# A long convolution through two half-size transforms at odd frequencies, with the last filter product stacked in fp32r

## The chip, the core and the metric

The kernel runs on one core of a Trainium2 chip. The metric is the device time of one execution in microseconds (us). It is one long program: a first transformer block, then two layers of a second block whose mixer has an attention branch and a long-convolution branch (hyena). Nearly all of its time is matrix work on TensorE (PE in the profile); the vector engine (DVE), the scalar engine (ACT) and the weight loads issued by SyncE (SP) work beside it.

## What is computed

The change touches the long convolution of the second block, which runs in layer 0 for two streams (the latent tokens and the context, 256 tokens each) and in layer 1 for one. Cut to what matters:

```python
def hyena_filter(length, fw1, fb1, fw2, fb2, fw3, fb3, fw4, freq):
    ...
    h = jnp.sin(freq[0] * (z @ fw1 + fb1))
    h = jnp.sin(freq[1] * (h @ fw2 + fb2))
    h = jnp.sin(freq[2] * (h @ fw3 + fb3))
    h = (h @ fw4).reshape(length, 2, HYENA_WIDTH)      # 64 -> 2 x 512 channels
    ...
    h = h * decay[:, None, :]
    return h[:, 0], h[:, 1]

def bidirectional_long_conv(v, h_fwd, h_bwd):
    length = v.shape[1]                                # 256
    n_fft = 2 * length
    k = jnp.concatenate([h_fwd, jnp.zeros((1, HYENA_WIDTH), h_fwd.dtype), h_bwd[:0:-1]], axis=0)
    v_f = jnp.fft.rfft(v.astype(jnp.float32), n=n_fft, axis=1)
    k_f = jnp.fft.rfft(k, n=n_fft, axis=0)
    return jnp.fft.irfft(v_f * k_f[None], n=n_fft, axis=1)[:, :length]

def hyena_mix(u, conv_w, conv_b, ..., bias):
    x0, x1, v = jnp.split(short_conv(u, conv_w, conv_b), 3, axis=-1)
    v = v * x1
    h_fwd, h_bwd = hyena_filter(length, ...)
    y = bidirectional_long_conv(v, h_fwd, h_bwd) + v.astype(jnp.float32) * bias
    return (y * x0).astype(u.dtype)
```

The filter depends on weights only, so its spectrum can be worked out long before the layer needs it.

## The kernel before

**Products.** Every large fp32 product is three fp32r matmuls: an operand is split into hi (an ACT copy that rounds to fp32r) and lo (a DVE subtract), and hi·hi, hi·lo and lo·hi are summed in PSUM. Weights come from DRAM as `raw` tiles of 512 KB (two k-tiles, issued on SP at L111); ACT copies each half to `whi` (L115), DVE makes `wlo` (L116). `gemm` (L126 to L128) and `gemm_T` (L139 to L141) use them. The pieces of the convolution go through `put`/`hilo` (L190 on ACT, L191 on DVE) and `mm3` (L215 to L217).

**The filter's spectrum.** `spectrum(layer)` is a generator. Three small fp32 matmuls `fm`, each followed by a sine (`sin`, 64 partitions x 256 points), give `sinh`. The last product with `fw4` (64 x 1024) is one fp32 matmul for each of two time halves and two directions (`hf` L763, `hb` L767); the trace shows such an fp32 matmul as two records. Then sums and differences are split into `hs` and `hd`, and `K` is their transform by the constant `F` (1024 columns: 256 cosines with the Nyquist row packed in, 256 sines): four products of six matmuls, and six more, `Kn`, for the Nyquist row. ACT or DVE evicts to `KR`, `KI`, and `KD` is `KR` with its first row exchanged. `spectrum_jobs` cuts the generator into 12 jobs; a background list releases them inside other matmul streams as these spend their columns. So spectrum 0 lies in the second feed-forward part of the first block (some 373 to 504 us), spectrum 1 in the feed-forward part of layer 0 (some 1205 to 1304 us).

**The convolution of a stream.** `hyena` makes three projections (`hy`), each followed by a three-tap convolution (`conv`: one ACT, two DVE instructions). `turn_v` transposes `vv` (`trv`, 8 transposes a stream) and splits it into `vTh`/`vTl`. `forward` transforms it: for each of two frequency halves m, real and imaginary part, 2 time halves x 3 matmuls into a `V` tile of 512 channels, 24 matmuls in all; DVE multiplies by `KR`, `KI`, `KD` and combines (L864 to L869, L854), and the four results are split into `Yh`/`Yl`. `inverse` is 48 matmuls `iy` of 256 columns with the constant `G`, and an elementwise end that gives `hyo`. Forwards run three times: twice in layer 0 (first matmuls at 615.9 and 649.8 us) and once in layer 1 (1384.6 us). Around them stand the gates' products (`ga`, `gh`) and, after the convolution, `oh` = hyo · w_o_hyena.

**What sets the order.** The kernel is written with tile pools; a scheduler fixes the order of each engine's instructions ahead of time by a model of its own. Each engine and the SP queue then run their row in that order and wait for semaphores. A tile pool bounds how far ahead a producer may run: 4 `raw` tiles, 16 `whi` and 16 `wlo`, 6 PSUM tiles for products (`mm`) and 2 for transposes and spectra (`tr`).

Of the kernel before, what the change touches and what calls it, by code (L numbers as in the profile page):

```python
# [42 lines left out]
class Net:  # L43
# [546 lines left out]
    def block1(self, nxt, before):  # L590
# [3 lines left out]
        self.fcols = self.const.tile([64, 12], F32, name="fcols")  # L594
# [128 lines left out]
    def sin(self, ps, b, fr):  # L723

        nc = self.nc
        x, n = self.k2("sarg", [64, 256]), self.k2("sn", [64, 256])
        nc.vector.tensor_scalar(out=x, in0=ps, scalar1=b, scalar2=fr, op0=ALU.add, op1=ALU.mult)
        nc.vector.tensor_scalar(out=n, in0=x, scalar1=1.0 / (2.0 * math.pi), scalar2=MAGIC, op0=ALU.mult, op1=ALU.add)
        nc.vector.tensor_scalar(out=n, in0=n, scalar1=MAGIC, scalar2=None, op0=ALU.subtract)
        for c in TWO_PI:  # L730
            nc.vector.scalar_tensor_tensor(out=x, in0=n, scalar=-c, in1=x, op0=ALU.mult, op1=ALU.add)
        nc.vector.tensor_scalar(out=x, in0=x, scalar1=PI_IN, scalar2=-PI_IN, op0=ALU.min, op1=ALU.max)
        h = self.k2("sinh", [64, 256])
# [3 lines left out]
    def spectrum(self, layer):  # L737

        nc, a = self.nc, self.a
# [9 lines left out]
        h = z  # L749
        for i in range(3):  # L750
            ps = self.tr("fm")
            nc.tensor.matmul(ps[:64, :256], w1 if i == 0 else w23[:, i - 1, :], h, start=True, stop=True)
            h = self.sin(ps[:64, :256], self.fcols[:, fc + i:fc + i + 1], self.fcols[:, fc + 3 + i:fc + 4 + i])
            yield
        dec = self.k4("dec", [P, 2, 512])
        nc.sync.dma_start(dec, a["decay"])
        F = self.const_pair("F", "dft")
        hs, hd = [self.pair(self.k4, x, [P, 2, 512]) for x in ("hs", "hd")]
        ALL = slice(None)
        for t in range(2):  # L760
            f, b = self.k2("f", [P, 512]), self.k2("b", [P, 512])
            ps = self.tr("hf")
            nc.tensor.matmul(ps, h[:, t * P:(t + 1) * P], w4[:, 0:512], start=True, stop=True)  # L763
# [3 lines left out]
            nc.tensor.matmul(ps, h[:, t * P:(t + 1) * P], w4[:, 512:1024], start=True, stop=True)  # L767
# [10 lines left out]
        KR, KI, KD = self.k4("KR", [P, 2, 512]), self.k4("KI", [P, 2, 512]), self.k2("KD", [P, 512])  # L778
        for m in range(4):
            ps = self.tr("K")  # L780
            src = hs if m < 2 else hd
            for t in range(2):
                self.mm3(ps, F, (ALL, slice(t * 512 + m * P, t * 512 + (m + 1) * P)), src, (ALL, t), t == 0, t == 1)
            if m == 2:
                nc.vector.tensor_scalar(out=KI[:, 0, :], in0=ps, scalar1=self.mask0, scalar2=None, op0=ALU.mult)
            else:
                nc.scalar.activation((KR if m < 2 else KI)[:, m % 2, :], ps, AF.Copy)
# [4 lines left out]
        nc.vector.tensor_copy(KD, KR[:, 0, :])  # L792
        nc.vector.tensor_copy(KD[:1, :], ps[:1, :])
        self.spectra[layer] = KR, KI, KD

    def spectrum_jobs(self, layer):
        g = self.spectrum(layer)
        return [(("spec", layer), lambda: next(g, None))] * 12

    def hyena(self, layer, X, between):  # L800
# [39 lines left out]
        KR, KI, KD = self.spectra[layer]  # L840
# [9 lines left out]
        def forward(vT):  # L850
# [5 lines left out]

            for m in range(2):
                V = [self.mm("V"), self.mm("V")]
                for q in range(2):
# [4 lines left out]
                nc.vector.tensor_tensor(out=t1, in0=V[0], in1=KR[:, m, :], op=ALU.mult)  # L864
                nc.vector.tensor_tensor(out=t2, in0=V[1], in1=KI[:, m, :], op=ALU.mult)
                comb(m, 0, t1, t2, ALU.subtract)
                t3, t4 = self.k2("y3", [P, 512]), self.k2("y4", [P, 512])
                nc.vector.tensor_tensor(out=t3, in0=V[0], in1=KI[:, m, :], op=ALU.mult)
                nc.vector.tensor_tensor(out=t4, in0=V[1], in1=KD if m == 0 else KR[:, 1, :], op=ALU.mult)  # L869
                comb(m, 1, t3, t4, ALU.add)  # L870
# [497 lines left out]
def dft_consts():  # L1368
    n = np.arange(256)[:, None]
    f = np.arange(256)[None]  # L1370
    th = 2 * np.pi * ((n * f) % 512) / 512
    fwd = np.concatenate([np.cos(th), -np.sin(th)], axis=1)
    fwd[:, 256] = (-1.0) ** np.arange(256)
    inv = 2 * fwd.T / 512
# [108 lines left out]
```

## Time and profile before

| | |
|---|---|
| median of 3 runs | 1786.92 us (1786.06 to 1790.84) |
| the profiled execution's own time | 1782.49 us |
| its span in the trace | 1780.7 us |
| PE busy | 1741.6 us, 98% of the span |
| DVE / ACT / PEld busy | 1238.5 / 864.3 / 1511.5 us |
| granted TensorE clock | full (0.998 in the mean) |

The profiled execution is 4.4 us faster than the median of the runs, so sums are made against 1782.49 and the difference is carried to the median. Matmul records overlap (their ends are modelled): the cost of one in a stream is the distance between starts, not the duration printed. The rows come further down, in groups.

### The profile page before, as it was taken

The numbers are of one execution on the slowest core, as the hardware profiler recorded it, in microseconds if no ns is written. First come the engines' busy times: TensorE is split into PE (matmuls) and PEld (weight loads), VectorE is DVE, ScalarE is ACT, GpSimd is POOL, SyncE is SP. The second block draws the span as 40 slices with busy tenths as digits, with TensorE's granted clock in tenths as the row PEclk, the third lists the DMA queues.
The fourth block names the chain that finished last, engine by engine and source line by source line (L and its number), as shares of the span: only waits on it lengthen the run. The fifth ranks groups of instructions, "written<-read, shape, count | busy, mean of one in ns | idle before, by whom it ended". The sixth has DMA issues, their size and how long they took to land.

```text
span 1780.7 us, 26970 instructions
## 1 busy us (share of the span) xinstructions
PE 1741.6 (98%) x9982; PEld 1511.5 (85%) x9982; DVE 1238.5 (70%) x2447; ACT 864.3 (49%) x1807; POOL 49.0 (3%) x77
## 2 busy tenths in 40 slices
PE   7999999999999999999999999999999999999998
PEld 5998887889888888888888888888789998989997
DVE  5855778886568887687667886456548857775554
ACT  6544557654467442356525433332336446565443
POOL 0000000000001000010000000000000001000000
PEclk9999999999999999999999999999999999999999
DMA  7757544675454428432545566454234554465553
GB/s 263 276 188 250 173 145 143 227 244 169 152 189 167 156 92 291 135 107 77 183 160 184 194 220 247 159 218 163 85 129 154 175 174 129 160 214 192 190 201 114
DMA packets 96244, 315.65 MB, mean 177 GB/s; under 512 B 10942, under 2 KB 18544, under 8 KB 96112
## 3 DMA queue, kind: packets, MB, share of 16 engines
q1 hardware_dynamic: 94176, 309.70, 51.1%
q10 hardware_dynamic: 1936, 4.23, 0.7%
q8 instruction: 78, 1.28, 0.3%
q14 instruction: 54, 0.44, 0.1%
HBM read 301.25 MB, written 12.63 MB: 176 GB/s over the span
## 4 chain that ended last, share of the span: by engine, by line
PE 83%; DMA 6%; DVE 6%; ACT 2%; issue 1%; POOL 1%; SPq 0%; POOLq 0%; ACTq 0%; DVEq 0%
PE f2u L139 3%; PE f2dn L126 3%; PE f2u L140 3%; PE f2u L141 3%; PE f2g L139 3%; PE f2g L140 3%; PE f2g L141 3%; PE f2dn L128 3%; PE f2dn L127 3%; DVE wlo L116 2%; PE O L1102 2%; PE trP L185 1%; PE oa L141 1%; PE oa L140 1%; PE oa L139 1%
## 5 line engine op out<-in xcount | busy, mean ns | idle before, releaser
L116 DVE TENSOR_TENSOR wlo<-raw,whi 128x512 fp32r<-128x512 f32 x844 | 546.4, 682 | 163.0 <-ACT whi L115 130.3
L115 ACT ACTIVATE whi<-raw 128x512 fp32r<-128x512 f32 x844 | 494.4, 624 | 164.6 <-PE f2dn L128 41.1
L648 DVE SCALAR_TENSOR_TENSOR wmod<-wmod,crow 128x1024 f32<-128x1024 f32 x96 | 116.0, 1218 | 1.0 <-DMA wmod<-in_w_modT_dram 0.6
L126 PE MATMUL f2dn<-whi,f2ah 128*128 128x512 f32 x264 | 103.7, 393 | 0.0
L139 PE MATMUL f2u<-fxh,whi 128*128 128x512 f32 (+1 forms) x304 | 103.2, 340 | 0.0
L139 PE MATMUL f2g<-fxh,whi 128*128 128x512 f32 (+1 forms) x304 | 103.2, 340 | 0.0
L141 PE MATMUL f2u<-fxh,wlo 128*128 128x512 f32 (+1 forms) x304 | 103.0, 339 | 0.0
L141 PE MATMUL f2g<-fxh,wlo 128*128 128x512 f32 (+1 forms) x304 | 103.0, 339 | 0.0
L140 PE MATMUL f2g<-fxl,whi 128*128 128x512 f32 (+1 forms) x304 | 103.0, 339 | 0.0
L140 PE MATMUL f2u<-fxl,whi 128*128 128x512 f32 (+1 forms) x304 | 103.0, 339 | 0.0
L128 PE MATMUL f2dn<-whi,f2al 128*128 128x512 f32 x264 | 102.8, 390 | 0.0
L127 PE MATMUL f2dn<-wlo,f2ah 128*128 128x512 f32 x264 | 102.8, 389 | 0.0
L648 DVE SCALAR_TENSOR_TENSOR mjunk<-wmod,crow 128x1024 bf16<-128x1024 f32 x64 | 77.5, 1218 | 22.0 <-DMA wmod<-in_w_modT_dram 18.3
L141 PE MATMUL hy<-lxh,wlo 128*128 128x256 f32 (+1 forms) x224 | 69.6, 315 | 0.1
L140 PE MATMUL hy<-lxl,whi 128*128 128x256 f32 (+1 forms) x224 | 69.7, 315 | 0.0
L139 PE MATMUL hy<-lxh,whi 128*128 128x256 f32 (+1 forms) x224 | 69.1, 315 | 0.0
L280 ACT ACTIVATE f2s<-f2g 128x512 f32<-128x512 f32 (+1 forms) x38 | 18.9, 496 | 99.5 <-PE f2g L141 99.5
L190 ACT ACTIVATE f2ah<-f2s 128x512 fp32r<-128x512 f32 (+1 forms) x40 | 21.3, 532 | 92.9 <-DVE f2s L283 92.9
L283 DVE TENSOR_TENSOR f2s<-f2u,f2s 128x512 f32<-128x512 f32 (+1 forms) x38 | 21.3, 562 | 63.4 <-PE f2u L141 63.4
L139 PEld LDWEIGHTS f2u<-fxh,whi 128*128 128x128 f32 x304 | 57.6, 190 | 7.6 <-issue 1.5
L139 PEld LDWEIGHTS f2g<-fxh,whi 128*128 128x128 f32 x304 | 57.7, 190 | 7.2 <-issue 0.9
L141 PEld LDWEIGHTS f2u<-fxh,wlo 128*128 128x128 f32 x304 | 57.7, 190 | 6.3
(520 smaller groups left out, 4809.1 us busy)
## 6 DMA issues: line engine op xcount, KB each, us to landing
wmod<-in_w_modT_dram SPq DMA_DIRECT2D x96, 512.0 KB, 5.9
raw<-in_ffn_w_gu_dram SPq DMA_DIRECT2D x88, 512.0 KB, 5.2
raw<-in_w_gate_up_dram SPq DMA_DIRECT2D x88, 512.0 KB, 5.7
raw<-in_w_in_dram SPq DMA_DIRECT2D x80, 512.0 KB, 4.4
raw<-in_ffn_w_down_dram SPq DMA_DIRECT2D x44, 512.0 KB, 5.1
raw<-in_w_down_dram SPq DMA_DIRECT2D x44, 512.0 KB, 4.0
raw<-in_w_out_dram SPq DMA_DIRECT2D x24, 512.0 KB, 4.7
raw<-in_w_in_q_dram SPq DMA_DIRECT2D x16, 512.0 KB, 3.8
```

The lines of the kernel that those rows point to most:

```text
L115: nc.scalar.activation(hi, raw[:, j], AF.Copy)
L116: nc.vector.tensor_tensor(out=lo, in0=raw[:, j], in1=hi.bitcast(F32), op=ALU.subtract)
L126: nc.tensor.matmul(ps[:, :n], xh, hi, start=first and k == 0, stop=False)
L127: nc.tensor.matmul(ps[:, :n], xh, lo, start=False, stop=False)
L128: nc.tensor.matmul(ps[:, :n], xl, hi, start=False, stop=last and k == z)
L139: nc.tensor.matmul(ps[:, m], hi[:, c], xh, start=first and k == 0, stop=False)
L140: nc.tensor.matmul(ps[:, m], hi[:, c], xl, start=False, stop=False)
L141: nc.tensor.matmul(ps[:, m], lo[:, c], xh, start=False, stop=last and k == z)
L190: nc.scalar.activation(hi, ps, AF.Copy)
L283: nc.vector.tensor_tensor(out=s, in0=pu[:, :W], in1=s, op=ALU.mult)
L648: nc.vector.scalar_tensor_tensor(out=junk, in0=w, scalar=1.0, in1=self.crows[s], op0=ALU.mult, op1=ALU.mult, accum_out=self.modc[layer][s] ...
L1102: nc.tensor.matmul(po[:, :256], V[:, kt, g * P:(g + 1) * P], pT[:, k, :], start=k == 0, stop=k == nt - 1)
```

## The change

The transform is taken at the odd frequencies, (k + 1/2) of 512, of which a real sequence of 256 has 256 and none is special: no Nyquist row, no mask, no `KD`. Even and odd samples are transformed separately at 128 frequencies, with 128 samples each; the value at frequency k and the one at its mirror image are the sum and the difference of the two halves. So a forward transform is 2 (real, imaginary) x 2 (even, odd) x 3 matmuls, and the same for each of `hs` and `hd`. `halves` joins the two: ACT copies the odd part out of PSUM (`odd`), DVE adds and subtracts. Transposes read `vv` with a stride of two samples; the constant `F` is 512 columns wide, its hi and lo in one tile.

The last filter product becomes fp32r: sine layer 3 runs on 128 partitions (its weights stand twice side by side), so that `h` stands twice; `hh` keeps hi in partitions 0 to 63 and lo in 64 to 127, and `w4`, loaded twice, one copy under the other, is split into hi and lo. Two matmuls, `hh` by w4 hi and by w4 lo, give (hi + lo) · (hi + lo). The spectrum becomes 11 jobs.

```diff
@@ const_pair
-        p = self.pair(self.k4, name, [P, D])
-        f = self.k4(name + "f", [P, D])
+        n = int(np.prod(self.a[src].shape[1:])) // 512
+        if n == 1:
+            both = self.k4(name, [P, 2, 512], F32R)
+            p = both[:, 0, :], both[:, 1, :]
+        else:
+            p = self.pair(self.k4, name, [P, n * 512])
+        f = self.k4(name + "f", [P, n * 512])
...
@@ spectrum
+        ws = [w1, w23[:, 0, :], w23[:, 1:3, :]]
         for i in range(3):
+            n = P if i == 2 else 64
             ps = self.tr("fm")
-            nc.tensor.matmul(ps[:64, :256], w1 if i == 0 else w23[:, i - 1, :], h, start=True, stop=True)
+            nc.tensor.matmul(ps[:n, :256], ws[i], h, start=True, stop=True)
...
+        hh = self.k2("hh", [P, 256], F32R)
+        nc.scalar.activation(hh, h, AF.Copy)
+        nc.vector.tensor_tensor(out=hh[64:], in0=h[64:], in1=hh[64:].bitcast(F32), op=ALU.subtract)
+        wp = self.pair(self.k4, "fw", [P, D])
...
+        for q in range(2):
+            c = slice(512 * q, 512 * q + 512)
+            self.put(wp, (slice(None), c), w4[:, c])
...
+        def filt(ps, t, q):
+            for i in range(2):
+                nc.tensor.matmul(ps, hh[:, t * P:(t + 1) * P], wp[i][:, q * 512:(q + 1) * 512], start=i == 0, stop=i == 1)
...
-            nc.tensor.matmul(ps, h[:, t * P:(t + 1) * P], w4[:, 0:512], start=True, stop=True)
+            filt(ps, t, 0)
...
-        KR, KI, KD = self.k4("KR", [P, 2, 512]), self.k4("KI", [P, 2, 512]), self.k2("KD", [P, 512])
-        for m in range(4):
-            ps = self.tr("K")
-            src = hs if m < 2 else hd
+        KR, KI = self.k4("KR", [P, 2, 512]), self.k4("KI", [P, 2, 512])
+        for q, (src, K) in enumerate(((hs, KR), (hd, KI))):
+            ps = [self.tr("K") for _ in range(2)]
             for t in range(2):
-                self.mm3(ps, F, (ALL, slice(t * 512 + m * P, t * 512 + (m + 1) * P)), src, (ALL, t), t == 0, t == 1)
...
+                self.mm3(ps[t], F, (ALL, slice(t * 256 + q * P, t * 256 + (q + 1) * P)), src, (ALL, t), True, True)
+            self.halves(K[:, 0, :], K[:, 1, :], ps[0], ps[1], q)
             yield
-        ps = self.tr("Kn")
-        for t in range(2):
-            self.mm3(ps[:1, :], F, (ALL, slice(t * 512 + 256, t * 512 + 257)), hs, (ALL, t), t == 0, t == 1)
...
+    def halves(self, a, b, even, odd, imag):
+        o = self.k2("odd", [P, 512])
+        nc.scalar.activation(o, odd, AF.Copy)
+        nc.vector.tensor_tensor(out=a, in0=even, in1=o, op=ALU.add)
+        if imag:
+            nc.vector.tensor_tensor(out=b, in0=o, in1=even, op=ALU.subtract)
+        else:
+            nc.vector.tensor_tensor(out=b, in0=even, in1=o, op=ALU.subtract)
@@ hyena, turn_v
-                    self.transpose(ps[:, ct * P:(ct + 1) * P], vv[ct][:, s * 256 + t * P:s * 256 + (t + 1) * P])
+                    self.transpose(ps[:, ct * P:(ct + 1) * P], vv[ct][:, s * 256:(s + 1) * 256].rearrange("p (l e) -> p e l", e=2)[:, t, :])
@@ hyena, forward
+            V = [[self.mm("V") for _ in range(2)] for _ in range(2)]
+            A = []
+            for q in range(2):
+                for t in range(2):
+                    o = t * 256 + q * P
+                    self.mm3(V[q][t], F, (ALL, slice(o, o + P)), vT, (ALL, t), True, True)
+            for q in range(2):
+                A.append([self.k2("y1", [P, 512]), self.k2("y2", [P, 512])])
+                self.halves(*A[q], *V[q], q)
             for m in range(2):
-                V = [self.mm("V"), self.mm("V")]
-                for q in range(2):
-                    for t in range(2):
-                        o = q * 256 + m * P
-                        self.mm3(V[q], F, (ALL, slice(t * 512 + o, t * 512 + o + P)), vT, (ALL, t), t == 0, t == 1)
-                t1, t2 = self.k2("y1", [P, 512]), self.k2("y2", [P, 512])
...
+                re, im = A[0][m], A[1][m]
                 t3, t4 = self.k2("y3", [P, 512]), self.k2("y4", [P, 512])
...
+                nc.vector.tensor_tensor(out=t3, in0=re, in1=KI[:, m, :], op=ALU.mult)
+                nc.vector.tensor_tensor(out=re, in0=re, in1=KR[:, m, :], op=ALU.mult)
+                nc.vector.tensor_tensor(out=t4, in0=im, in1=KI[:, m, :], op=ALU.mult)
+                comb(m, 0, re, t4, ALU.subtract)
+                nc.vector.tensor_tensor(out=im, in0=im, in1=KR[:, m, :], op=ALU.mult)
+                comb(m, 1, t3, im, ALU.add)
```

The order changes near these pieces only. On ACT around the forward transform of layer 1, before (from the split of the transposed `vv` to the last `Yh`; `x_...` is the three-tap convolution of the third projection):

```order
L190 ACTIVATE vTh<-trv 128x512 x2
L813 ACTIVATE x_14020<-hy,cols 128x256
L115 ACTIVATE whi<-raw 128x512 x4
L190 ACTIVATE Yh<-y_14181 128x512
L813 ACTIVATE x_14020<-hy,cols 128x256
L190 ACTIVATE Yh<-y_14188 128x512
L190 ACTIVATE Yh<-y_14209 128x512
L190 ACTIVATE Yh<-y_14216 128x512
```

and after:

```order
L190 ACTIVATE vTh<-trv 128x512 x2
L839 ACTIVATE x_13990<-hy,cols 128x256
L115 ACTIVATE whi<-raw 128x512 x3
L815 ACTIVATE odd<-V 128x512
L115 ACTIVATE whi<-raw 128x512
L815 ACTIVATE odd<-V 128x512
L839 ACTIVATE x_13990<-hy,cols 128x256
L115 ACTIVATE whi<-raw 128x512 x2
L190 ACTIVATE Yh<-y_14153 128x512
L190 ACTIVATE Yh<-y_14165 128x512
L190 ACTIVATE Yh<-y_14154 128x512
L190 ACTIVATE Yh<-y_14177 128x512
```

Two `odd` copies are new, the first of them behind three `whi` copies; all four `Yh` now stand behind six `whi` copies where the first stood behind four.

On DVE at the same place, before (from the first product with the spectrum):

```order
L864 TENSOR_TENSOR y_14181<-V,KR 128x512
L865 TENSOR_TENSOR y_14182<-V,KI 128x512
L868 TENSOR_TENSOR y_14188<-V,KI 128x512
L854 TENSOR_TENSOR y_14181<-y_14181,y_14182 128x512
L869 TENSOR_TENSOR y_14189<-V,KD 128x512
L864 TENSOR_TENSOR y_14209<-V,KR 128x512
L191 TENSOR_TENSOR Yl<-y_14181,Yh 128x512
```

and after:

```order
L816 TENSOR_TENSOR y_14153<-V,odd 128x512
L820 TENSOR_TENSOR y_14154<-V,odd 128x512
L816 TENSOR_TENSOR y_14159<-V,odd 128x512
L818 TENSOR_TENSOR y_14160<-odd,V 128x512
L895 TENSOR_TENSOR y_14165<-y_14153,KI 128x512
L897 TENSOR_TENSOR y_14166<-y_14159,KI 128x512
L896 TENSOR_TENSOR y_14153<-y_14153,KR 128x512
L899 TENSOR_TENSOR y_14159<-y_14159,KR 128x512
L880 TENSOR_TENSOR y_14153<-y_14153,y_14166 128x512
L880 TENSOR_TENSOR y_14165<-y_14165,y_14159 128x512
```

Four additions and subtractions stand ahead of the first product, and the first combination (L880, L854 before) is the ninth instruction instead of the fourth.

On SP somewhat later in layer 1 (`spill` stores a gate's tile to DRAM; the numbers tell tiles apart), before:

```order
L1205 DMA spill_14318<-Ta_14316 128x256
L1205 DMA spill_14347<-Ta_14345 128x256
L1205 DMA spill_14376<-Ta_14374 128x256
L111 DMA raw_14519<-in_w_o_hyena_dram 128x1024
L1205 DMA spill_14405<-Ta_14403 128x256
L111 DMA raw_14529<-in_w_o_hyena_dram 128x1024
```

and after:

```order
L1235 DMA spill_14284<-Ta_14282 128x256
L1235 DMA spill_14313<-Ta_14311 128x256
L1235 DMA spill_14342<-Ta_14340 128x256
L1235 DMA spill_14371<-Ta_14369 128x256
L111 DMA raw_14485<-in_w_o_hyena_dram 128x1024
L111 DMA raw_14495<-in_w_o_hyena_dram 128x1024
```

The first load of w_o_hyena stands behind the fourth spill instead of the third.

## Rows read from the trace of the kernel before

**Rows 1.** The page's parts 1 and 4: busy time; the chain that ended last.

```profile
PE 1741.6 (98%) x9982; PEld 1511.5 (85%) x9982; DVE 1238.5 (70%) x2447; ACT 864.3 (49%) x1807; POOL 49.0 (3%) x77
...
PE 83%; DMA 6%; DVE 6%; ACT 2%; issue 1%; POOL 1%; SPq 0%; POOLq 0%; ACTq 0%; DVEq 0%
```

**Rows 2.** Waits of PE: waiter, releaser: us in total, times, longest.

```profile
PE trm L185 <- DVE ffn1n L697: 10.2, 2, 9.8
```

**Rows 3.** Windows: us, busy (count) of PE, PEld, DVE, ACT, POOL, clock, DMA, GB/s.

```profile
400.00:440.00 40.00, 40.00 (x306) 36.81 (x305) 26.32 (x52) 19.27 (x41) 0.00 (x0) 1.00 0.48 160
600.00:640.00 40.00, 38.38 (x200) 32.74 (x199) 33.55 (x58) 14.86 (x26) 0.00 (x0) 1.00 0.36 117
1260.00:1310.00 50.00, 50.00 (x215) 39.00 (x214) 20.07 (x32) 15.22 (x26) 0.00 (x0) 1.00 0.27 89
1370.00:1420.00 50.00, 48.61 (x375) 46.63 (x375) 45.68 (x89) 27.37 (x55) 0.00 (x0) 1.00 0.46 150
```

**Rows 4.** PE's timeline in spectrum 0, one product K: start, duration, instruction.

```profile
458.06 0.39 PE L215 MATMUL K<-hsh,Fh 128*128 128x512 f32 x1
...
459.42 0.39 PE L126 MATMUL ffn2dn<-whi,ffn2ah 128*128 128x512 f32 x1
```

**Rows 5.** Instructions of single tiles: count, duration ns min/median/max, first and last start.

```profile
L215 PE MATMUL K<-hsh,Fh x8: 389/389/389, 458.1 to 1284.1; 128*128 128x512 f32 x8
...
L215 PE MATMUL V<-vTh,Fh x24: 389/389/497, 615.9 to 1390.2; 128*128 128x512 f32 x24
...
L763 PE MATMUL hf<-fw,sinh x8: 589/641/693, 415.0 to 1265.8; 64*128 64x512 f32 x8
...
L185 PEld LDWEIGHTS trv<-ident,vv x24: 138/140/144, 607.5 to 1381.6; 128*128 128x128 f32 x24
```

**Rows 6.** PE's timeline around one product hf of spectrum 0 and of spectrum 1.

```profile
414.71 0.28 PE L140 MATMUL ffn2u<-ffn2l,whi 128*128 128x256 f32 x1
414.83 0.28 PE L141 MATMUL ffn2u<-ffn2h,wlo 128*128 128x256 f32 x1
415.04 1.12 PE L763 MATMUL hf<-fw,sinh 64*128 64x512 f32 x2
...
416.31 0.28 PE L140 MATMUL ffn2u<-ffn2l,whi 128*128 128x256 f32 x1
...
1252.14 0.39 PE L128 MATMUL f2dn<-whi,f2al 128*128 128x512 f32 x1
...
1253.85 0.39 PE L127 MATMUL f2dn<-wlo,f2ah 128*128 128x512 f32 x1
```

**Rows 7.** PE's timeline, the Nyquist product Kn of spectrum 0.

```profile
500.81 0.40 PE L215 MATMUL Kn<-hsh,Fh 128*1 128x512 f32 x1
...
502.20 0.28 PE L139 MATMUL ffn2u<-ffn2h,whi 128*128 128x256 f32 x1
```

**Rows 8.** Groups by line and shape, DVE, 600 to 660 us: busy, mean ns, idle before.

```profile
L854 DVE TENSOR_TENSOR y<-y,y 128x512 f32<-128x512 f32 x7 | 4.8, 682 | 0.0
```

**Rows 9.** Timelines of DVE and of PE, layer 0: last Yl, first iy.

```profile
629.52 0.69 DVE L191 TENSOR_TENSOR Yl<-y,Yh 128x512 fp32r<-128x512 f32 x1
...
633.12 0.28 PE L215 MATMUL iy<-Gh,Yh 128*128 128x256 f32 x1
```

**Rows 10.** ACT's timeline in layer 1; in brackets idle before and its releaser.

```profile
1388.40 1.15 ACT L115 ACTIVATE whi<-raw 128x512 fp32r<-128x512 f32 x2 [1.06 <-DMA raw<-in_w_in_dram]
...
1397.85 0.63 ACT L190 ACTIVATE Yh<-y 128x512 fp32r<-128x512 f32 x1 [1.56 <-DVE y L854]
```

**Rows 11.** PE's timeline in layer 1: end of V, first iy, start and end of gh's part.

```profile
1390.63 0.39 PE L217 MATMUL V<-vTh,Fl 128*128 128x512 f32 x1
1390.86 0.28 PE L139 MATMUL hy<-lxh,whi 128*128 128x256 f32 x1
...
1398.29 0.28 PE L215 MATMUL iy<-Gh,Yh 128*128 128x256 f32 x1
...
1410.29 0.28 PE L139 MATMUL gh<-lxh,whi 128*128 128x256 f32 x1
...
1419.54 0.28 PE L139 MATMUL oh<-hyoh,whi 128*128 128x256 f32 x1
```

**Rows 12.** SP's timeline in layer 1: the fourth spill, the last load of w_o_hyena.

```profile
1407.89 0.32 SPq L1205 DMA_DIRECT2D spill<-Ta  x1
1408.31 0.38 SPq L111 DMA_DIRECT2D raw<-in_w_o_hyena_dram  x1
```

More of the change, by code (lines that the diff above doesn't have):

```diff
@@ L199, in const_pair @@
     def const_pair(self, name, src):
-        p = self.pair(self.k4, name, [P, D])
-        f = self.k4(name + "f", [P, D])
+        n = int(np.prod(self.a[src].shape[1:])) // 512
[5 more added lines that the diff above has]
+        f = self.k4(name + "f", [P, n * 512])
         self.nc.sync.dma_start(f, self.a[src].rearrange("p a b -> p (a b)"))
-        for q in range(2):
+        for q in range(n):
             c = slice(512 * q, 512 * q + 512)
@@ L593, in block1 @@
         hs = {}
-        self.fcols = self.const.tile([64, 12], F32, name="fcols")
+        self.fcols = self.const.tile([P, 12], F32, name="fcols")
         for t in range(2):
@@ L742, in spectrum @@
         nc.sync.dma_start(w1, a["filt_w1"][layer])
-        w23 = self.k2("fw23", [64, 2, 64])
+        w23 = self.k2("fw23", [64, 3, 64])
         nc.sync.dma_start(w23, a["filt_w23"][layer])
-        w4 = self.k4("fw4", [P, D])[:64, :]
+        w4 = self.k4("fw4", [P, D])
         nc.sync.dma_start(w4, a["filt_w4"][layer])
@@ L766, in spectrum @@
             ps = self.tr("hb")
-            nc.tensor.matmul(ps, h[:, t * P:(t + 1) * P], w4[:, 512:1024], start=True, stop=True)
+            filt(ps, t, 1)
             if t == 0:
@@ L777, in spectrum @@
             yield
[L778 to L781 removed]
+        KR, KI = self.k4("KR", [P, 2, 512]), self.k4("KI", [P, 2, 512])
+        for q, (src, K) in enumerate(((hs, KR), (hd, KI))):
+            ps = [self.tr("K") for _ in range(2)]
             for t in range(2):
[L783 to L794 removed]
+                self.mm3(ps[t], F, (ALL, slice(t * 256 + q * P, t * 256 + (q + 1) * P)), src, (ALL, t), True, True)
+            self.halves(K[:, 0, :], K[:, 1, :], ps[0], ps[1], q)
+            yield
+        self.spectra[layer] = KR, KI
+    def halves(self, a, b, even, odd, imag):
+        nc = self.nc
+        o = self.k2("odd", [P, 512])
[5 more added lines that the diff above has]
+            nc.vector.tensor_tensor(out=b, in0=even, in1=o, op=ALU.subtract)
     def spectrum_jobs(self, layer):
         g = self.spectrum(layer)
[L798 removed]
+        return [(("spec", layer), lambda: next(g, None))] * 11
     def hyena(self, layer, X, between):
@@ L839, in hyena @@
         self.need(("spec", layer))
-        KR, KI, KD = self.spectra[layer]
+        KR, KI = self.spectra[layer]
         def turn_v(s):
@@ L1368, in dft_consts @@
 def dft_consts():
[L1369 to L1374, printed above, removed]
-    inv[0] /= 2
-    inv[256] /= 2
-    part = lambda x: np.ascontiguousarray(x.reshape(-1, P, x.shape[1]).transpose(1, 0, 2).astype(np.float32))
-    return part(fwd), part(inv)
+    th = 2 * np.pi * (np.arange(P) + 0.5) / 512
+    n = np.arange(256).reshape(P, 2).T
+    fwd = np.stack([np.concatenate([np.cos(n[p][:, None] * th), -np.sin(n[p][:, None] * th)], axis=1) for p in range(2)], axis=1)
+    t = np.arange(256)[None]
+    thm = [th[:, None], np.pi - th[:, None]]
+    inv = np.stack([f(m * t) / 256 for f in (np.cos, lambda x: -np.sin(x)) for m in thm], axis=1)
+    return np.ascontiguousarray(fwd.astype(np.float32)), np.ascontiguousarray(inv.astype(np.float32))
 def hyena_consts():
```

31 lines of the change are left out of this document (14 added, 17 removed).

## The prediction, written before the run

> **What bounds the kernel now.** The page first: PE is busy for 98% of the span, and the chain that ended last runs 83% through PE, 6% through DVE and 6% through transfers [rows 1]. The list of PE's waits next: the largest is 10.2 us in two places where a feed-forward part begins, far from this change, and no wait of the spectra stands in the list [rows 2]. Then the stretches that the change touches, as windows: around spectrum 0 and spectrum 1 PE is busy for all of 40.00 and 50.00 us while DVE is busy for 26.32 and 20.07; around the first forwards of layer 0 PE has 38.38 of 40, DVE 33.55; around the forward of layer 1 PE has 48.61 of 50 and DVE 45.68 [rows 3]. The granted clock is 1.00 in all four. So in the spectra a matmul taken away is worth its distance to the next start, nearly certainly. In layer 0 DVE has some slack, in layer 1 hardly any: there the saving may be taken back by DVE, ACT or a transfer.
>
> **The price of a matmul.** The six matmuls of a K product start at 458.06 and the next matmul after them at 459.42: 1.36 / 6 = 0.2267 us each [rows 4]. The printed 389 ns overlap.
>
> **What goes, term by term.** (1) K: before, 48 matmuls in two layers (8 in each of the six groups of which one is shown [rows 5]); the change makes 2 x 2 x 3 a layer, 24 in all. 24 x 0.2267 = 5.44 us. (2) V: 72 matmuls (three groups of 24 [rows 5]) become 36: 36 x 0.2267 = 8.16. (3) The Nyquist product goes: 500.81 to 502.20 is 1.39 [rows 7], twice: 2.78. (4) The last filter product: from 414.83 to 416.31 stand hf and two matmuls of 256 columns at the 0.12 of 414.71 to 414.83, so 1.48 - 0.24 = 1.24; from 1252.14 to 1253.85 stand hf and two of 512 columns, 1.71 - 0.45 = 1.26 [rows 6]. Eight such products at 1.25; the new one is two fp32r matmuls of 512 columns, which I price like K's, 0.453: 8 x 0.797 = 6.37. They are new in one respect, operands whose partitions 64 to 127 hold another part of the same number; TensorE reads 128 rows there as in K. Sum: 22.75 us.
>
> **What comes in.** DVE: each forward has 16 elementwise steps instead of 12 (12 products and combinations before, 4 joins more), 12 in all; a spectrum has some 3 more (joins, the split of w4 and of `hh` against the splits of F and the Nyquist copies), 6; the two constants F of the layers need one split less each, -2. 16 x 0.68 [rows 8] = 10.9 us, on an engine that is idle for 13.7 of 40 us in spectrum 0 and 29.9 of 50 in spectrum 1 [rows 3]. In the spectra I cost them at nothing: PE's own work around hides them, and in the new order K stands 40 rows (some 9 us) behind the last hb as before in spectrum 0, 22 rows (5 us) in spectrum 1. If that cover were gone, 6 x 0.68 = 4.1 us. The sine step on 128 partitions has as many columns as on 64: nothing; fm with 128 columns of weights, 0.1. w4 is 256 KB more to load, twice, F 256 KB less, four times: nothing, all of it long before use.
>
> The transposes read every second sample. No row prices a strided weight load: it lies between nothing and a doubled load, 24 x 0.138 [rows 5] = 3.3 us. I take nothing, since the nearest rows, loads of 0.138 that run beside the matmul ahead, are hidden, and keep 3.3 for the range. The Trainium skill (Advanced Engine Details and Errata, SBUF Cachelines) says that reads need two hits on a 16-byte line to go at full rate; two fp32 samples at a stride of two lie on one line, so by it nothing is lost and the sum would stay; no run here shows it yet.
>
> **The forwards of layer 0.** The new chain is longer: ACT copies the odd part, four joins, then products. On before's clock the last Yl began at 629.52 and the first iy at 633.12 [rows 9], 3.6 us of slack. The new order gives the third and fourth Yh a place behind eight whi copies and three-tap convolutions on ACT; stepping through it with durations of this trace puts the last Yh at some 633.6 where PE, 2.72 us ahead after 12 removed matmuls, wants it at about 633.2. I take 0.5 for this forward and 0.1 for the second: of 5.44 us some 4.8 stay. Bounds: 0 and all of it.
>
> **The forward of layer 1.** Here the saving is 2.72: V would end at 1388.1 where now it does at 1390.86 [rows 11]. But the first odd copy stands behind the third whi copy, and that pair waits for its load until 1388.40 [rows 10]; so the copies end at 1389.5 and 1390.7, and the joins and products run from there at 0.60 a step (16 steps of DVE, with two three-tap steps of the last hy between). The third Yh comes at some 1400.2; PE wants it, with iy at 1398.29 [rows 11] drawn forward to 1397.0, for the seventh iy, at 1397.7. That is a stall of 2.5 us, and some 0.6 more for wlo splits that stand behind: more than the saving at that point. After it come ga, gh and oh, and these wait for weights: both loads of w_o_hyena stand behind the fourth spill on SP [rows 12], whose gate tile on ACT stands behind two whi copies that wait for loads. gh, which began at 1410.29, begins at about 1410.8; its part, which ended at 1419.54 with waits for wlo and w_o_hyena in it [rows 11], ends at 1418.1 to 1419.1, since some of the waits there are for transfers that start as early as before. I take 0.9 us kept and 1.8 lost; bounds: 2.72 kept, and 2 lost beyond it if the later load of w_o_hyena holds the whole stretch.
>
> Sum: 22.75 - 0.5 - 0.1 - 1.8 - 0.1 = 20.2 us. The profiled execution took 1782.49, so 1762.3 against it; the median of the runs shown is 1786.92, 0.25% higher, and from it 1766.7. A measurement of this kernel can tell about 0.3%, 5.4 us, from no change.
>
> **Rivals.** (a) The forwards give nothing: DVE and ACT chains and the loads take back all 8.16, in layer 0 too. For it: DVE's 45.68 of 50 in layer 1 [rows 3], and the step-through above, which already ends late in two places. Against: DVE's idle share in layer 0 and 3.6 us of slack. Then only terms 1, 3 and 4 are left: 14.6 - 0.1, 1772.4 us; with 2 us lost beyond that in layer 1, 1774.4. (b) The stacked product is not cheaper than the fp32 one, because the two-part operand is slow: without 6.37, 1773.1. Against it: TensorE takes any fp32r operand of 128 x 512 in this trace at 0.2267. (c) The strided loads cost 3.3: 1770.0. (d) A matmul in such a stream is really worth less than its distance, since TensorE could go faster and something else spaces it. With each of the 60 removed K and V matmuls and the 12 of Kn at 0.13, the savings would be 7.0 less, 1773.7. The rows speak against it: six in a row at 0.2267, beside neighbours at the same distance, with nothing waited for. The Trainium skill (TensorE: Matmul & The Clock Gate, Back-to-back issue gap) states some 131 ns for each matmul of 512 columns in a stream with weight loads; the trace has 227 and decides. (e) No change: in the spectra the weight copies and not PE set the pace, and PE is busy only because its records stretch; then the savings turn into waits for whi there, and with the forwards lost the time stays at 1786.9. Against: no wait of PE for whi in those windows [rows 2, 3]. (f) Slower: DVE sets the end wherever the change puts joins, PE's savings are hidden, and the 16 added steps lie on the path in full: 1786.9 + 10.9 = 1797.8. It decides from the point at which DVE is busy for the whole of such a window; it is now at 20 to 34 of 40 to 50 outside layer 1 [rows 3], so only there could it happen, for 4 x 0.68 = 2.7 us.
>
> **How the numbers follow.** Chances: forecast 0.64; (a) 0.18; (b) 0.03; (c) 0.07; (d) 0.01; (e) 0.04; (f) 0.02; the costs of the forwards nil, all 22.7 kept, 1764.2, 0.01. Predicted: 1766.7. Its own range goes by the bounds of its costs, 1764.2 to 1770, and by the spread of medians (the three runs span 1786.06 to 1790.84) 2 to 3 us lower at the foot. The range that should hold 8 in 10 takes in (a), (b), (c) and (d) above: 1761 to 1776. Faster by over 0.3%: all but (e) and (f), 0.94; within it 0.04; slower 0.02.
>
> **What would show it.** Right: K's 12 matmuls a layer at 0.227 with no wait; hf as two records 0.227 apart; PE idle by some 3 us more around iy of layer 1, a wait for Yh; the stretch of layer 0 some 5 us shorter. Wrong: hf records that are longer than K's (b); trv's weight loads clearly over 138 ns and later starts behind them (c); a new wait of PE for `odd`, Yh or wlo of over 3 us in layer 0 (a); a wait for hs or whi in the spectra (e).

## The result

The changed kernel takes 1765.13 us (median of 4 runs, 1764.57 to 1766.28) against 1786.49 for the kernel before on the same chip (median of 4 runs, 1785.28 to 1790.84): a ratio of 0.9883, 95% interval 0.9864 to 0.9902, 17.5 to 24.3 us. Forecast were 1766.7 us and a range of 1761 to 1776.

The page's busy times after, with the span of 1762.8 us (before: [rows 1]):

```profile
PE 1720.6 (98%) x9910; PEld 1502.3 (85%) x9910; DVE 1244.7 (71%) x2463; ACT 866.4 (49%) x1813; POOL 48.8 (3%) x77
```

PE has 21.0 us less to do in 72 matmul records fewer (the eight fp32 products had two records each and now have two matmuls each, so only K, V and Kn count), DVE has 16 instructions more, as counted, for 6.2 us (10.9 were allowed). PE's waits after, the first row of the list and three further down (columns as in [rows 2]):

```profile
PE trm L185 <- DVE ffn1n L702: 10.6, 2, 10.2
...
PE iy L220 <- ACT Yh L190: 1.9, 1, 1.9
...
PE gh L141 <- DVE wlo L116: 0.9, 1, 0.9
...
PE oh L139 <- ACT whi L115: 0.5, 1, 0.5
```

The last three stand in layer 1 and are new. A wait of PE for `vv` ahead of the transposes in layer 0 is gone; it stood in the list of before:

```profile
PE trv L185 <- DVE vv L835: 1.6, 1, 1.6
```

**The terms.** One product K after (PE's timeline, as [rows 4]), and one last product in each spectrum:

```profile
462.94 0.39 PE L220 MATMUL K<-hsh,F 128*128 128x512 f32 x1
...
464.30 0.39 PE L126 MATMUL ffn2dn<-whi,ffn2ah 128*128 128x512 f32 x1
```

```profile
423.52 0.40 PE L782 MATMUL hf<-fwh,hh 128*128 128x512 f32 x1
423.75 0.40 PE L782 MATMUL hf<-fwl,hh 128*128 128x512 f32 x1
423.99 0.28 PE L139 MATMUL ffn2g<-ffn2h,whi 128*128 128x256 f32 x1
...
1250.59 0.39 PE L782 MATMUL hf<-fwh,hh 128*128 128x512 f32 x1
1250.82 0.39 PE L782 MATMUL hf<-fwl,hh 128*128 128x512 f32 x1
1251.04 0.39 PE L139 MATMUL f2u<-fxh,whi 128*128 128x512 f32 x1
```

K keeps its 1.36 us for six matmuls, and there are half as many. The stacked product takes 0.47 and 0.45 us where the fp32 one took 1.24 and 1.26 [rows 6].

**Where the time came from, by stage.** The order of PE is the same in both kernels but for the pieces that changed and the transposes of layer 1, which run a few products `hy` earlier, so the start of one and the same matmul can be compared in two traces. The table gives what a trace gained on the trace of before in each stretch (the stretches by the clock of before, us), for a second execution of the kernel before (e4), two executions of the changed kernel (the second is e12), the half-size transform alone (e2) and the stacked product alone (e6). It is worked out from the start times in the traces. The cut at 1378 lies ahead of the transposes of layer 1. At 1381, the cut that the expectations of e7, e8 and e10 use, traces with the changed order still have eight short matmuls (0.9 us) to do that before has done, so that their losses behind it look 0.9 us too large.

| stretch of before | before again | changed | changed again | transform alone | stack alone |
|---|---|---|---|---|---|
| 0 to 413, nothing changed | 4.23 | 0.79 | 0.69 | 0.80 | 0.90 |
| 413 to 540, spectrum 0 | 0.07 | 6.93 | 6.77 | 3.34 | 2.66 |
| 540 to 606 | 0.0 | 0.0 | 0.0 | 0.0 | 0.0 |
| 606 to 615, transposes of layer 0 | -2.70 | 1.74 | 1.74 | 1.74 | 0.54 |
| 615 to 675, both forwards of layer 0 | 0.0 | 5.05 | 5.04 | 5.06 | 0.0 |
| 675 to 1225, nothing changed | -0.86 | -1.55 | -1.22 | -0.78 | -0.47 |
| 1225 to 1304, spectrum 1 | 0.0 | 7.40 | 7.40 | 4.11 | 3.30 |
| 1304 to 1378 | -0.17 | -0.47 | -1.71 | 0.47 | -0.39 |
| 1378 to 1421, forward and gates of layer 1 | -2.03 | -0.65 | -0.35 | -0.36 | -0.72 |
| 1421 to the end | -0.48 | -1.31 | -0.41 | -1.60 | -0.15 |
| whole span | -1.95 | 17.92 | 17.95 | 12.78 | 5.67 |

The second column is the yardstick: two executions of one program differ by 4 us over the first 413 us, by 1 to 3 us where PE waits, and by less than 0.1 where PE is never idle. The gains of the spectra and of layer 0 stand clear of that, to 0.2 us alike in two executions. Layer 1 gained nothing on the first trace of before. From trace to trace the gain is 17.9 us and from median to median 21.4, since the execution of before that was profiled (1782.49) lies 4 us under its median and those of the changed kernel (1764.57 and 1764.55) lie 0.6 and 0.8 us under theirs.

### The profile page after: what moved, and what is told of

The parts are those of the page before. It is cut to its first block, busy times and chain, and to the rows that moved or that the text cites. A ratio compares the mean times of both kernels' runs of the same rounds, so it can differ in the third digit from the quotient of the medians.

```text
span 1762.8 us, 26817 instructions
## 1 busy us (share of the span) xinstructions
PE 1720.6 (98%) x9910; PEld 1502.3 (85%) x9910; DVE 1244.7 (71%) x2463; ACT 866.4 (49%) x1813; POOL 48.8 (3%) x77
## 3 DMA queue, kind: packets, MB, share of 16 engines
q10 hardware_dynamic: 2000, 4.23, 0.7%
## 4 chain that ended last, share of the span: by engine, by line
PE 74%; issue 11%; DVE 6%; DMA 5%; ACT 2%; POOL 1%; SPq 0%; POOLq 0%; ACTq 0%; DVEq 0%
PE f2u L140 3%; PE f2u L141 3%; PE f2u L139 3%; PE f2dn L128 3%; PE f2dn L126 3%; PE f2g L140 3%; PE f2g L141 3%; PE f2dn L127 3%; PE f2g L139 3%; PE O L1132 2%; DVE wlo L116 2%; PE q L126 1%; PE q L128 1%; PE q L127 1%; PE trP L185 1%
## 5 line engine op out<-in xcount | busy, mean ns | idle before, releaser
L140 PEld LDWEIGHTS f2g<-fxl,whi 128*128 128x128 f32 x304 | 57.7, 190 | 6.3
```

Of the source, the lines that this page charges most:

```text
L140: nc.tensor.matmul(ps[:, m], hi[:, c], xl, start=False, stop=False)
```

## The experiments

**e1 and e6, the stacked product alone.** Both are the kernel before with the new last product. The first has 13 jobs for each spectrum, since the splits of w4 end with a break of their own; the second leaves that break out and has 12, as before.

```diff
-            nc.tensor.matmul(ps, h[:, t * P:(t + 1) * P], w4[:, 0:512], start=True, stop=True)
+            filt(ps, t, 0)
...
-        return [(("spec", layer), lambda: next(g, None))] * 12
+        return [(("spec", layer), lambda: next(g, None))] * 13
```

> The kernel before with the stacked fp32r last filter product alone (transform, Nyquist row and transposes as before). Theory (the terms add, PE sets the pace in the spectra): each of the eight products costs 0.45 us instead of 1.25, so spectrum 0 and spectrum 1 each end 3.2 us earlier, 6.4 us in all, 1780 us beside 1786.5. Rival (the two-part operand is no cheaper, or the extra splits stall the spectrum): nothing, 1786.5, and a PE wait for hh or fw in the spectra.

Measured: ratio 0.9984 (0.997 to 0.9999), some 3 us, between theory and rival. The trace shows where. In spectrum 0 e1 gained 4.5 us on before up to 505 us, 1.4 of it because the Nyquist product had not run yet, and lost 4.5 again between 540 and 606. The Nyquist product's first start, before and in e1 (rows of the tile Kn; first and last start):

```profile
L215 PE MATMUL Kn<-hsh,Fh x4: 392/397/397, 500.8 to 1303.1; 128*1 128x512 f32 x4
```

```profile
L215 PE MATMUL Kn<-hsh,Fh x4: 392/395/397, 574.6 to 1361.1; 128*1 128x512 f32 x4
```

The thirteenth job came too late for the stream in which the others run; Kn ran 74 us later, inside the projections of layer 0, and the jobs queued behind it slipped too. Besides Kn's 1.4 us the stretch holds a wait of PE of 1.3 us for `lxh` that before does not have, and the granted clock was 0.57 from 566 to 570 us, which takes up to 1.7 us; so not all of the loss is shown to be the break's. With spectrum 1 the same break cost nothing: from 1225 to the first `gh` (1410) the trace of e1 gained 3.0 us and that of e6 2.5. For e6, with one line less:

```diff
             self.put(wp, (slice(None), c), w4[:, c])
-        yield
```

> The kernel before with the stacked last product, as e1, but in 12 jobs, as before, instead of 13: one break between jobs is left out. Theory: in e1 the thirteenth job pushed the Nyquist product out of the stream and the modulation's jobs behind it, and that took back what the product gave; here the product gives 3.2 us in each spectrum, nothing is taken back in the stretch up to 606 us, and the kernel is 5 to 7 us faster than before, 1780. Rival (what e1 lost is due to the added splits of w4 and hh): as in e1, some 0 to 3 us.

Measured: ratio 0.9975 (0.9966 to 0.9985), 2.7 to 6.1 us; the table has 2.66 us in spectrum 0, 3.30 in spectrum 1 and nothing lost from 540 to 606. The two stretches make 5.96 us, inside the theory's 5 to 7; the total (4.5 us at the ratio of 0.9975) lies under it, with an interval that reaches into it. The product is worth what the rows said. The break cost some 3 us up to 606 us in one trace; the totals of e1 and e6 can't be told apart, since their intervals meet.

**e2, the half-size transform alone.**

```diff
-            filt(ps, t, 0)
+            nc.tensor.matmul(ps, h[:, t * P:(t + 1) * P], w4[:, 0:512], start=True, stop=True)
```

> The changed kernel with the old fp32 last product. Theory: K and the Nyquist row give 4.1 us in each spectrum, the two forwards of layer 0 give 2.7 each, the forward of layer 1 nothing or a loss of 1 to 2: 12 to 14.5 us below before, 1772 to 1774.5. With e1 the two savings add up to that of the whole change within 2 us. Rival (the parts share a bottleneck): this alone gives less than 10 or more than 17 us.

Measured: 1771.64 against 1786.32, ratio 0.9923 (0.9904 to 0.9941), 13.8 us. In spectrum 1 it gained 4.11 us and e6 gained 3.30; the whole change gained 7.40 there: the parts add. In spectrum 0 they make 6.0 against 6.93 and 6.77, and no run says where the rest comes from. Over the whole span the traces of e2 and e6 make 18.45 us, the whole change 17.92. The ratios of e1 and e2 make 16.6 us beside 20.9 for the change, not within the 2 us expected.

**e3, transposes without the stride.**

```diff
-vv[ct][:, s * 256:(s + 1) * 256].rearrange("p (l e) -> p e l", e=2)[:, t, :]
+vv[ct][:, s * 256 + t * P:s * 256 + (t + 1) * P]
```

> The changed kernel with the transposes reading 128 neighbouring samples instead of every second one, so that the two halves of the transform get the wrong samples; the order of all instructions stays. Theory: the weight loads of the 24 transposes fall from 209 ns to the 138 of before, and the time stays within 0.5 us, since the distance between two transposes (0.12 us) stays. Rival (strided loads cost their added 71 ns each): 1.7 us faster, 0.57 in each forward's transposes.

Weight loads of the transposes, changed kernel and e3 (before: the last of [rows 5]):

```profile
L185 PEld LDWEIGHTS trv<-ident,vv x24: 195/209/220, 599.8 to 1361.2; 128*128 128x128 f32 x24
```

```profile
L185 PEld LDWEIGHTS trv<-ident,vv x24: 138/140/144, 601.5 to 1362.8; 128*128 128x128 f32 x24
```

The stride makes a load half as long again, 209 ns instead of 140, and costs nothing: from 606 to 615 us e3 gained 1.82 us on before and the changed kernel 1.74, and both forwards' matmuls start at the same distances. Its total, 1767.3 us (ratio 0.9897, 0.9876 to 0.9918), is no shorter than the changed kernel's.

**e4, the kernel before once more.** No edit.

> The kernel before once more, for a second trace of it: how far two executions of one program differ by stage. Theory: the wait of PE for vv in layer 0 (1.62 us, released by DVE, which had waited 1.81 us for a load of wmod) is a matter of when that load lands and is not in every execution, so that the 1.74 us by which the changed kernel is shorter there is no part of the change. Rival: the wait is here too, at the same length, and the change took it away.

Measured: ratio 1.0006 (0.9992 to 1.0019). The wait for vv is here again and longer, so my theory falls:

```profile
606.60 0.77 PE L185 MATMUL trv<-ident,vv 128*128 128x128 f32 x5 [2.68 <-DVE vv L835]
```

and the stretches around it, windows of e4 (columns as in [rows 3]):

```profile
600.00:606.00 6.00, 3.92 (x19) 3.02 (x17) 5.97 (x11) 0.78 (x1) 0.00 (x0) 1.00 0.62 182
606.00:612.00 6.00, 5.40 (x19) 4.38 (x20) 3.15 (x5) 1.09 (x2) 0.00 (x0) 0.72 0.43 168
```

The wait is 1.06 us longer than in the first trace, yet the stretch is 2.70 us longer: behind the wait the granted clock is 0.72 in the mean, that is at its lower level (1.2 GHz) for some of the window. The clock also made most of the other difference between the two traces of before, in layer 1 (before, then e4):

```profile
1411.00:1421.00 10.00, 9.01 (x69) 8.21 (x68) 8.28 (x18) 5.92 (x13) 0.00 (x0) 1.00 0.82 265
```

```profile
1411.00:1422.00 11.00, 9.95 (x65) 9.24 (x65) 8.45 (x19) 6.05 (x13) 0.00 (x0) 0.84 0.80 267
```

Up to 1417 us the two are level to 0.1 us there, and 1.5 us apart at 1421.

**e5, twelve jobs in the changed kernel.**

```diff
-        return [(("spec", layer), lambda: next(g, None))] * 11
+        return [(("spec", layer), lambda: next(g, None))] * 12
```

> The changed kernel with 12 background jobs for each spectrum instead of 11; the twelfth does nothing, but the jobs that stand behind the spectrum in the background list (the parts of the modulation, wmod) come one place later, as in the kernel before. Theory: the wait of PE for vv in layer 0 went because the modulation's jobs moved one place forward, so that no piece of it waits for a load ahead of the last three-tap convolutions on DVE; here the wait comes back, 1 to 2.7 us, and the rest stays. Rival (it went because one split of F less stands ahead of it on DVE): no wait of over 0.3 us.

Measured: 1764.75 us, no wait for vv, 1.58 us gained from 606 to 615 as in the changed kernel. The theory of the jobs' places falls as well.

**e9, F as wide as before.** What the traces still had in common: with the wide F, two weight loads stand on SP between G and the first load of wmod in layer 0, with the narrow one a single load.

```diff
     r["dft"], r["idft"] = dft_consts()
+    r["dft"] = np.concatenate([r["dft"]] * 2, axis=1)
```

> The changed kernel with the constant F as wide as before: 1024 columns in DRAM, of which the second 512 are a copy that no product reads, so that F is again 512 KB, two splits and two tiles; the number of jobs stays at 11. In the order of SP two weight loads stand again between G and the first load of wmod in layer 0, where the changed kernel has one. Theory: that place on SP is why the wait of PE for vv went; here wmod lands late, DVE waits for it 1 us or more, and PE waits for vv by 1 to 2.7 us; the time is 1 to 3 us over that of the changed kernel. Rival (something else in the half-size transform took the wait away): no wait for vv.

SP's timeline behind G in before, in the changed kernel and in e9 (start, duration, instruction):

```profile
578.82 0.42 SPq L203 DMA_DIRECT2D Gf<-in_idft_dram  x1
588.24 1.52 SPq L111 DMA_DIRECT2D raw<-in_w_in_dram  x2
589.81 0.43 SPq L634 DMA_DIRECT2D wmod<-in_w_modT_dram  x1
```

```profile
571.11 0.42 SPq L208 DMA_DIRECT2D Gf<-in_idft_dram  x1
579.18 0.33 SPq L111 DMA_DIRECT2D raw<-in_w_in_dram  x1
579.55 0.43 SPq L639 DMA_DIRECT2D wmod<-in_w_modT_dram  x1
```

```profile
572.78 0.42 SPq L208 DMA_DIRECT2D Gf<-in_idft_dram  x1
582.37 1.53 SPq L111 DMA_DIRECT2D raw<-in_w_in_dram  x2
583.94 0.43 SPq L639 DMA_DIRECT2D wmod<-in_w_modT_dram  x1
```

DVE's timeline and PE's waits of e9:

```profile
591.43 1.23 DVE L653 SCALAR_TENSOR_TENSOR mjunk<-wmod,crow 128x1024 bf16<-128x1024 f32 x1 [1.73 <-DMA wmod<-in_w_modT_dram]
```

```profile
PE trv L185 <- DVE vv L861: 1.7, 1, 1.7
```

The load of wmod is issued 11.2 us behind G instead of 8.4; DVE stands 1.73 us for it with the last three-tap convolutions behind it, and PE waits 1.7 us for vv. So it is the width of F that took the wait away: all five traces with the wide F (before twice, e1, e6, e9) have it, 1.1 to 2.7 us, and none of the nine with the narrow one. SP's order is 1.2 of the 2.7 us by which wmod's load comes later, the distance between the two weight loads; the other 1.5 lie ahead of the first weight load (9.6 us behind G against 8.1), and what holds that one was not tested. The total is 1770.36 us (ratio 0.9915, 0.9899 to 0.993), 5 us over the changed kernel on the same chip (e12), more than the 1 to 3 expected, though the two intervals overlap: from 606 to 615 us e9 lost 0.20 where the changed kernel gained 1.74, and from 1378 to 1421 it lost 5.0 against 0.4 to 0.7. In the latter the clock fell (0.76 in the mean from 1395 to 1409), as it did in e3, e4 and e7 with the one F or the other; so that part is not shown to be the width's.

**e7, the removed TensorE work put back in layer 1.**

```diff
+            if S == 1:
+                ps = self.tr("spare")
+                for i in range(4):
+                    self.mm3(ps, F, (ALL, slice(0, P)), vT, (ALL, 0), i == 0, i == 3)
```

> The changed kernel with 12 matmuls of 512 columns more in layer 1, right behind the V product, into a PSUM tile that nobody reads: the 2.72 us of TensorE work that the change removed there. Theory: PE does not set the pace there; the wait for Yh (1.9 us) shrinks to nothing, and the part up to 1421 us before ends at most 1.0 us later. Rival (PE sets the pace, the wait is of no account): it ends 2.7 us later. The same part ended 1.65 us apart in two executions of the kernel before, so the wait for Yh decides and not the end alone.

PE's waits in layer 1, 1360 to 1406 us of e7, all of them:

```profile
PE gh L141 <- DVE wlo L116: 2.1, 2, 1.5
PE oh L139 <- ACT whi L115: 1.3, 1, 1.3
```

No wait for Yh is left. From 1378 to the first gh (1410 us of before) e7 lost 0.44 us, the changed kernel 0.81 with a lower clock behind its wait, and e12 gained 0.13 at full clock: 2.72 us more work, and it came at most 0.6 us later. The forward of layer 1 is not set by PE's work. The end of the stretch fits neither theory nor rival: e7 lost 4.8 us more up to 1421, for behind the start of gh it waited longer (the two rows; 0.9 and 0.5 us in the changed kernel), and the clock fell there, too. Windows of e7:

```profile
1394.00:1401.00 7.00, 3.56 (x21) 2.86 (x20) 4.74 (x12) 2.98 (x7) 0.00 (x0) 0.86 0.54 197
1401.00:1408.00 7.00, 7.00 (x43) 7.00 (x42) 4.39 (x8) 2.78 (x6) 0.00 (x0) 0.65 0.84 255
```

The clock divides the traces. Between gh and 1421 every one in which it fell there lost 1.4 us or more (e4 1.4, e3 2.0, e1 3.0, e9 3.8, e7 4.8), and the eight others that were compared (the changed kernel, e2, e5, e6, e8, e10, e11, e12) lie between 0.5 lost and 0.3 gained. For e3, with the changed kernel's own order:

```profile
1398.00:1404.00 6.00, 5.16 (x30) 5.07 (x30) 4.65 (x9) 4.04 (x8) 0.00 (x0) 0.72 0.63 207
```

The totals of e7 (1765.43; the profiled execution, 1770.28, was its longest) and of the changed kernel are the same.

**e8, no joins in layer 1.**

```diff
-                self.halves(*A[q], *V[q], q)
+                if S == 2:
+                    self.halves(*A[q], *V[q], q)
...
+                rv, iv = (re, im) if S == 2 else (V[0][m], V[1][m])
```

> The changed kernel without the joins in layer 1: the odd copies and the four additions and subtractions are left out there, and the products take even and odd parts as they are. Theory (the chain is too long by the joins): the third Yh comes 3 us earlier, the wait of PE for Yh falls from 1.9 to under 0.3 us; the part up to 1421 us before still ends less than 2 us earlier, since oh waits for the loads of w_o_hyena. Rival (Yh is late because the whi copies ahead of it on ACT wait for their loads): a wait for Yh of over 1.3 us stays.

PE's waits in layer 1, 1358 to 1404 us of e8:

```profile
PE oh L141 <- DVE wlo L116: 1.4, 2, 1.0
PE iy L222 <- DVE Yl L191: 0.4, 1, 0.4
PE iy L220 <- ACT Yh L190: 0.3, 1, 0.3
PE ga L139 <- DVE y L898: 0.2, 1, 0.2
```

The wait for Yh fell from 1.9 to 0.3 us, and the stretch from 1378 to 1421 gained 0.5 us on before where the changed kernel lost 0.4 to 0.7: theory on both counts; the total is 1763.67 us. So the joins make the one long wait. But without them the saved 2.72 us are still not to be had: up to the first gh e8 gained 0.35 us where e12 gained 0.13. Several short hold-ups behind y, Yh and Yl take the place of the long wait (PE's starts there are 2.5 us further apart in sum than at 0.12 us each, 2.7 in e12), so the rest of the chain holds PE, too.

**e10 and e11, the spills of Ta on ACT.** In layer 1 alone, and in both layers:

```diff
-            Ta[4 * n + f] = self.spill(g, W)
+            Ta[4 * n + f] = self.spill(g, W, nc.scalar if last else None)
```

> The changed kernel with the four spills of Ta in layer 1 issued by ACT, right behind the instruction that makes the tile, instead of by SP. Theory: in layer 1 the part behind the forward waits for the loads of w_o_hyena, which stand on SP behind the fourth spill; without it they are issued 2 to 4 us earlier, ACT's wait of 3.0 us for w_o_hyena falls under 1 us, and the part from 1381 to 1421 us before ends 1 to 2.5 us earlier than in the changed kernel (1.5 to 4.0 us of loss in five traces of its order or near it). The total falls by as much, too little to tell alone. Rival (the loads wait for a free raw tile, not for the spills): no earlier issue, no gain.

> As e10, with the spills of Ta on ACT in layer 0 too (eight more). Theory: layer 0 has no wait for w_o_hyena, so it gains nothing more than e10, within 1 us, and loses nothing either as long as ACT has the time. Rival (issuing from ACT delays its whi copies): a new wait of PE for whi in layer 0 and 1 to 3 us lost.

**e12, the changed kernel again**, on the same chip.

> The changed kernel once more, beside the two variants with spills on ACT, for its time on the same chip and a second trace. Theory: 1764 to 1766 us, a wait for Yh of 1.8 to 2.3 us in layer 1 and a wait of ACT for w_o_hyena of 3 to 4 us. Rival (the late w_o_hyena was a matter of the one execution): ACT's wait under 1 us.

ACT's first wait for w_o_hyena in layer 1, in the changed kernel, in e12 and in e10:

```profile
1393.98 0.63 ACT L115 ACTIVATE whi<-raw 128x512 fp32r<-128x512 f32 x1 [3.00 <-DMA raw<-in_w_o_hyena_dram]
```

```profile
1394.85 0.63 ACT L115 ACTIVATE whi<-raw 128x512 fp32r<-128x512 f32 x1 [1.80 <-DMA raw<-in_w_o_hyena_dram]
```

```profile
1395.57 1.15 ACT L115 ACTIVATE whi<-raw 128x512 fp32r<-128x512 f32 x2 [0.24 <-DMA raw<-in_w_o_hyena_dram]
```

Without the spills ahead of them the loads are issued 0.8 us behind the first Ta instead of 3.3, and ACT's first wait for them goes to 0.24 us (0.78 in e11). The rival, a wait for a free raw tile, falls. In e12 ACT's first wait was 1.80 us, neither the 3 to 4 expected there nor the rival's under 1. The stretch from 1378 to 1421 gained 0.2 us in both against 0.65 and 0.35 lost: 0.5 to 0.9 us better, less than the 1 to 2.5 expected and no more than traces of one kernel differ; DVE's wlo is next (PE still waits 0.6 and 0.4 us for it behind the start of gh in e10). In e11 no wait of PE for whi appeared in layer 0, so its rival falls, too. The totals, 1765.85 (ratio 0.9892, 0.9875 to 0.991) and 1762.91 (0.9878, 0.9865 to 0.9892) beside 1765.33 for e12 (0.9896, 0.9877 to 0.9914), can't be told apart; e11 has the lowest median of all, but a version that beats the changed kernel is not shown.

## Why the prediction was right

**The price of a matmul and the four removed terms: right.** K and Kn at 0.2267 and 1.39 make 4.11 us a spectrum, and e2 gained 4.11 in spectrum 1. The last product at 1.25 less 0.453 makes 3.19, and e6 gained 3.30. Together 7.30, measured 7.40 twice; in spectrum 0 6.93 and 6.77, where 0.4 and 0.5 were lost between 505 and 540 us. V in layer 0 is worth 5.44, and 5.05 stayed. No wait for hs, hh, fw or the odd copies of K appeared in the spectra.

**The forwards of layer 0: right, a little too dear.** I took 4.8 us; the stretch kept 5.05. No wait of PE is to be seen in it.

**The forward of layer 1: the mechanism right, its size off.** The stall came where it was put, at the first part of iy, for Yh, released by ACT: 1.86 us where I had 2.5 and 0.6 of wlo splits behind it. The later half was mis-sized, as far as the traces can tell: I let the part end 0.9 us earlier than before, and it ended 0.4 to 0.7 later than in one trace of before and 1.4 to 1.7 earlier than in the other, whose clock fell at the end. What I had not priced is the clock. PE's window after the stall in the changed kernel, and in e12:

```profile
1380.00:1384.00 4.00, 4.00 (x22) 4.00 (x22) 4.00 (x7) 0.63 (x1) 0.00 (x0) 0.57 0.13 19
```

```profile
1381.00:1385.00 4.00, 3.66 (x29) 3.46 (x30) 4.00 (x8) 0.63 (x1) 0.00 (x0) 1.00 0.10 12
```

22 matmuls instead of 29 in four microseconds. In the first the matmuls from 1380.39 to 1383.59 start 0.21 us apart where their neighbours are at 0.12: in four microseconds at 0.57 of full clock (1 - 0.57) x 4 = 1.7 us of PE's work are lost, behind a wait of 1.86. Against e12, where the clock stayed up, 0.9 us of that is left at the first gh, in part since PE waited 0.34 us more there for a wlo of ga. Behind that start e12 waited 1.64 us for a wlo of gh, and at 1421 the two are 0.3 us apart.

**Costed at nothing, and wrong: the width of F.** "F 256 KB less, four times: nothing, all of it long before use" is the step that failed. The narrower F brought wmod's load forward, in part by moving it ahead of one weight load on SP, and that took away a wait of 1.62 us (2.68 in the other trace) on PE's path, 1.74 us of gain. It made good the 1.3 to 1.6 us by which layer 1, on the first trace of before, fell short of the sum, and that is luck: the stretches that the change touches give 20.5 and 20.6 us in the two traces, beside my 20.2. The stretches in which nothing changed took 2.5 to 2.7 us back, so that the traces differ by 17.9 and 18.0. And the profiled execution of before was 4 us under its median: I carried that distance over to the changed kernel, whose own was 0.6 under. The two nearly cancel in the median, and that is luck, too.

**The rivals.** (a) falls for layer 0 and holds for layer 1. (b) falls to the rows of hf. (c): the loads are longer and still cost nothing (e3). By the Trainium skill (Advanced Engine Details and Errata, SBUF Cachelines) a stride of two fp32 should have read at full rate; the trace has 209 against 140 ns, and the measurement decides. (d) falls: the removed matmuls were worth their 0.227 us, not the 0.131 that the Trainium skill (TensorE: Matmul & The Clock Gate, Back-to-back issue gap) states. (e) and (f) fall: no wait for whi in the spectra, and in the spectra and in layer 0 no wait of PE came with the added DVE steps; the four of layer 1 are part of the chain that holds PE there (e8).

**Left open:** why executions of the kernel before lie between 1779 and 1791 us when its stages agree so well where PE is busy, and what decides whether the clock falls behind a wait.

## What to carry to other kernels

Where PE is busy for the whole of a stretch, a removed matmul is worth its distance to the next start, and such terms add; where another chain ends the stretch, as in layer 1, the same 12 matmuls were worth next to nothing, and putting them back cost at most 0.6 us up to the gates. A smaller constant or one more break between background jobs can move what stands behind it in a program whose order is planned ahead. That was worth 1.7 us one way (F) and some 3 us the other (e1 against e6 up to 606 us, up to 1.7 of it the clock's); read the order on SP for every load that the edit touches. A wait of PE can cost more than its own length, through the clock behind it: 0.9 us more behind a wait of 1.86 (against e12), 1.64 more in e4. When two traces are compared by stages, cut where both have done the same work, and read the granted clock of each stage before its length.

## What the runs showed of the hardware

After a wait of PE of about two microseconds the granted clock went to its lower level for some microseconds in some executions and not in others: after 1.86 us for Yh in the changed kernel (0.57 in the mean of the next four) but not after 1.80 in e12; after 2.68 us for vv in the second trace of before (0.72 in the mean of the next six), while the first trace, with 1.62 us, had 1.00 in the window [rows 3]. It fell behind shorter waits as well: in e4 behind two of 0.42 and 0.55 us (0.84 from 1411 to 1422). I had forecast with a clock of 1.00.

A transposing matmul's weight load from every second fp32 sample took 209 ns against 140 for neighbouring ones, hidden behind the matmul ahead.
